# Moving the direct columns of a row pair from behind to ahead of its second bf16 products

## Chip, cores, metric

One core of one Trainium2 chip. The metric is the device time of one execution in microseconds.

## The reference, cut to what matters

```python
def reference(x, w_qkv):              # x: (16, 512, 768) f32, w_qkv: (768, 2304) f32
    qkv = np.matmul(x, w_qkv)
    ...                               # q, k, v = thirds of the last axis
    return np.stack([q, k, v], axis=0)
```

So it is one matrix product of 8192 x 768 by 768 x 2304, stored in another arrangement.

## The kernel before

The rows are worked in 32 pairs of 128-row blocks; "pair" below means such a pair of row blocks. After three pairs of start-up, 28 pairs go through `two` and the last one through `last`. Of the 2304 columns, 2048 are two "quads" (`a` and `b`: a pair of row blocks by a pair of 512-column blocks), computed by a Winograd form of Strassen's scheme with seven block products instead of eight. The remaining 256 are the "direct columns", computed plainly by `rem`. Products 1 and 2 run in bf16; products 3 to 7 use f32 operands made of sums (`float32r`).

```python
def product(u, n, ps, start):                  # three matmuls of 512 columns
    ...
    for j in range(KH):                        # KH = 3
        nc.tensor.matmul(ps[:], lhs[j], rhs[j], start=(start and j == 0), ...)

def do(u, n):
    ...
    if n == 1:
        u.x = bank(); product(u, 1, u.x, True)
        nc.scalar.activation(c11, u.x[:], ident)
    elif n == 2:
        u.z = bank(); product(u, 2, u.z, True)
        nc.vector.tensor_tensor(c11, c11, u.z[:], op=add)
    elif n == 6:
        product(u, 6, u.x, False)              # adds to product 1
        nc.scalar.activation(c12, u.x[:], ident)
    ...

def rem_row(p, r, ps):                         # six matmuls of 256 columns
    for j in range(KT):
        nc.tensor.matmul(ps, xb[p][:, j, r * P:(r + 1) * P], w_rem[:, j, :], ...)

def rem(p):                                    # the direct columns of a pair
    ps = ps_pool.tile([P, 2, REM], fp32, name="ps")
    for r in range(2):
        rem_row(p, r, ps[:, r, :])
    o = or_pool.tile([P, 2, REM], fp32, name="orem")
    nc.scalar.activation(o[:], ps[:], ident)
    nc.sync.dma_start(rows_of(1, p, R_OFF - H, R_OFF - H + REM), o[:])

def two(a, b, early):
    do(a, 1); do(b, 1)
    early()                                    # next pair: transpose, cast, sums; loads of the one after
    do(a, 2); do(b, 2)
    rem(a.p)
    do(a, 6); do(b, 6)
    do(a, 5); do(a, 7); do(b, 5); do(b, 7)
    do(a, 4); do(a, 3); store_quad(a)
    do(b, 4); do(b, 3); store_quad(b)
```

On TensorE a pair is therefore 12 bf16 matmuls of 512 columns, 12 bf16 matmuls of 256 columns and 30 f32 matmuls of 512 columns.

## Time and profile before

| | before |
|---|---|
| median time, first three runs | 363.31 us (363.23 to 363.45) |
| span of the profile | 362.0 us |
| TensorE busy | 98% |
| period of a pair in the steady loop | 10.76 us |
| the 54 matmuls of a pair at their own steps (a step: from one matmul's start to the next one's) | 10.70 us |

The views that carry the argument are shown in the prediction. Beside them belongs the table by stretches, here two pairs of the loop. Its columns are the stretch, its length, then for each engine the busy time with the number of instructions, the granted clock, the DMA's busy share and GB/s.

```profile
206.87:217.63 10.76, 10.69 (x54) 7.83 (x55) 6.78 (x8) 5.38 (x9) 5.86 (x6) 1.00 0.95 294
217.63:228.39 10.76, 10.69 (x54) 7.82 (x55) 6.77 (x8) 5.39 (x9) 5.85 (x6) 1.00 0.90 293
```

TensorE fills 10.69 of 10.76 us, and every pair looks like the next one. VectorE, ScalarE and GpSimd have 4 to 5 us free in each. ScalarE's idle time stands ahead of these evictions (groups of instructions: count, busy us and mean ns, idle us before them with what ended it):

```profile
L266 ACT ACTIVATE orem<-ps 128x512 f32<-128x512 f32 x31 | 18.6, 601 | 56.3 <-PE ps L256 54.3
...
L227 ACT ACTIVATE o<-ps 128x512 f32<-128x512 f32 x58 | 34.7, 599 | 6.6 <-PE ps L206 1.5
```

L266 evicts the direct columns and waits for TensorE 54.3 us in all.

### The profile page before, as it was taken

The page shows a single profiled execution, that of the slowest core. Times are in us where ns is not written, and L with a number is a line of the kernel's source. Part 1 is how long each engine was busy: PE and PEld are TensorE (multiplying, and loading weights), DVE is VectorE, ACT ScalarE, POOL GpSimd, SP SyncE. Part 2 cuts the span into 40 slices and gives each one's busy share as a digit, 9 for nine tenths or more (in the row PEclk, how much of TensorE's full clock was granted, in tenths as well). Part 3 has the DMA queues.
Part 4 walks back from the last instruction along what each step waited for, and adds up shares of the span by engine and source line. Part 5 has one row for each costly group of instructions (what it writes and reads, how often), then busy time and mean ns, then how long its engine had stood idle before and what let it go on. Part 6 is the DMA issues. An engine that isn't in the chain of part 4 may idle for free.

```text
span 362.0 us, 5220 instructions
## 1 busy us (share of the span) xinstructions
PE 353.5 (98%) x1765; PEld 248.6 (69%) x1797; DVE 224.4 (62%) x239; ACT 182.5 (50%) x304; POOL 174.1 (48%) x180
## 2 busy tenths in 40 slices
PE   8999999999999999999999999999999999999995
PEld 3644577777777776777777777777777777777763
DVE  3489746865566765566675565676556676556642
ACT  4547554445454545454545544444545454545452
POOL 0000960756664445664445665444666444666410
PEclk9999999999999999999999999999999999999999
DMA  7999969999999989899899999899989998989766
GB/s 295 381 381 339 346 224 343 331 304 298 278 321 298 295 275 295 282 313 313 284 277 294 281 306 316 281 283 285 295 284 317 295 295 274 300 275 332 266 251 242
DMA packets 80617, 108.08 MB, mean 299 GB/s; under 512 B 4816, under 2 KB 60368, under 8 KB 80592
## 3 DMA queue, kind: packets, MB, share of 16 engines
q1 hardware_dynamic: 65184, 96.35, 82.5%
q10 hardware_dynamic: 15408, 11.41, 9.7%
q8 instruction: 14, 0.23, 0.3%
q14 instruction: 11, 0.09, 0.1%
HBM read 32.24 MB, written 75.50 MB: 298 GB/s over the span
## 4 chain that ended last, share of the span: by engine, by line
PE 96%; ACT 1%; issue 1%; ACTq 0%; DVE 0%
PE ps L206 75%; PE ps L256 11%; PE ps L382 9%; PE ps L362 1%; PE ps L161 1%; ACT o L237 0%; ACTq L297 0%; ACT xb L141 0%; ACT orem L311 0%; DVE xb L139 0%; ACT xc L141 0%; ACTq L313 0%; DVE zero L340 0%; ACTq L311 0%
## 5 line engine op out<-in xcount | busy, mean ns | idle before, releaser
L206 PE MATMUL ps<-t,s 128*128 128x512 f32 x696 | 171.4, 395 | 0.0
L206 PEld LDWEIGHTS ps<-t,s 128*128 128x128 f32 x696 | 128.5, 188 | 26.5
L169 POOL CAST xb<-xf 128x1536 bf16<-128x1536 f32 x29 | 43.9, 1514 | 168.5 <-DVE xf L124 159.1
L234 DVE TENSOR_TENSOR o<-o,ps 128x512 f32<-128x512 f32 x58 | 39.9, 689 | 91.8 <-ACT o L233 91.8
L124 DVE STREAM_TRANSPOSE xf<-xin 128x1536 f32<-128x1536 f32 x29 | 85.5, 2950 | 5.7 <-DMA xin<-in_x_dram 2.9
L206 PE MATMUL ps<-b,xb 128*128 128x512 bf16 x320 | 74.2, 379 | 1.9
L206 PEld LDWEIGHTS <-xb 128*128 128x128 bf16 x348 | 31.7, 98 | 41.6 <-issue 7.3
L233 ACT ACTIVATE o<-ps 128x512 f32<-128x512 f32 x58 | 34.7, 598 | 44.7 <-PE ps L206 44.7
L240 DVE TENSOR_TENSOR o<-o,ps 128x512 f32<-128x512 f32 x58 | 39.9, 688 | 21.4 <-PE ps L206 20.2
L206 PE MATMUL ps<-b,s 128*128 128x512 f32 x174 | 48.7, 389 | 0.0
L256 PE MATMUL ps<-w_rem,xb 128*128 128x256 bf16 x384 | 47.2, 273 | 0.0
L266 ACT ACTIVATE orem<-ps 128x512 f32<-128x512 f32 x31 | 18.6, 601 | 56.3 <-PE ps L256 54.3
L237 ACT ACTIVATE o<-ps 128x512 f32<-128x512 f32 x58 | 34.7, 598 | 24.2 <-PE ps L206 21.4
L220 ACT ACTIVATE o<-ps 128x512 f32<-128x512 f32 x58 | 34.6, 597 | 23.8 <-DVE o L240 20.7
L256 PEld LDWEIGHTS <-xb 128*128 128x128 bf16 x384 | 37.4, 98 | 11.2 <-issue 0.5
L227 ACT ACTIVATE o<-ps 128x512 f32<-128x512 f32 x58 | 34.7, 599 | 6.6 <-PE ps L206 1.5
L224 DVE TENSOR_TENSOR o<-o,ps 128x512 f32<-128x512 f32 x58 | 36.4, 668 | 2.0 <-ACT o L220 1.3
L206 PEld LDWEIGHTS ps<-b,s 128*128 128x128 f32 x174 | 32.6, 188 | 6.9
L178 POOL TENSOR_TENSOR s<-s,xf 128x384 fp32r<-128x384 f32 x29 | 30.1, 1039 | 2.3
L177 POOL TENSOR_TENSOR s<-xf 128x384 fp32r<-128x384 f32 x29 | 31.0, 1069 | 0.0
L179 POOL TENSOR_TENSOR s<-xf 128x384 fp32r<-128x384 f32 x29 | 29.5, 1017 | 0.0
L181 POOL TENSOR_TENSOR s<-xf,s 128x384 fp32r<-128x384 f32 x29 | 29.5, 1016 | 0.0
(36 smaller groups left out, 129.3 us busy)
## 6 DMA issues: line engine op xcount, KB each, us to landing
out_dram<-o SPq DMA_DIRECT2D x62, 768.0 KB, 5.3
out_dram<-o SPq DMA_DIRECT2D x65, 256.0 KB, 4.5
xin<-in_x_dram SPq DMA_DIRECT2D x62, 192.0 KB, 6.7
xin<-in_x_dram ACTq DMA_DIRECT2D x54, 192.0 KB, 4.5
out_dram<-orem SPq DMA_DIRECT2D x31, 256.0 KB, 5.1
st<-in_w_qkv_dram SPq DMA_DIRECT2D x6, 768.0 KB, 14.1
xin<-in_x_dram SPq DMA_DIRECT2D x3, 768.0 KB, 5.7
st<-in_w_qkv_dram SPq DMA_DIRECT2D x6, 256.0 KB, 6.2
```

Source lines behind the costliest of these rows:

```text
L124: nc.vector.transpose(t[:].rearrange("p j (g b) -> p g j b", b=G), xin.pop(p)[:].rearrange("p g (a j) -> p g j a", a=G),)
L169: nc.gpsimd.tensor_copy(out=xb[p][:], in_=xf[p][:])
L206: nc.tensor.matmul(ps[:], lhs[j], rhs[j], start=(start and j == 0), stop=(j == KH - 1), skip_group_check=True,)
L220: nc.scalar.activation(c11, u.x[:], ident)
L224: nc.vector.tensor_tensor(c11, c11, u.z[:], op=add)
L227: nc.scalar.activation(c12, u.x[:], ident)
L233: nc.scalar.activation(c22, u.x[:], ident)
L234: nc.vector.tensor_tensor(c22, c22, u.y[:], op=add)
L237: nc.scalar.activation(c21, u.x[:], ident)
L240: nc.vector.tensor_tensor(c12, c12, u.y[:], op=add)
L256: nc.tensor.matmul(ps, xb[p][:, j, r * P:(r + 1) * P], w_rem[:, j, :], start=(j == 0), stop=(j == KT - 1), skip_group_check=True,)
L382: nc.tensor.matmul(ps[n][:], xb[p][:, j, r * P:(r + 1) * P], w[:, j, :], start=(j == 0), stop=(j == KT - 1), skip_group_check=True,)
```

## The change

The direct columns go between the first and the second bf16 products. One line moves:

```diff
         do(a, 1)
         do(b, 1)
         early()
+        rem(a.p)
         do(a, 2)
         do(b, 2)
-        rem(a.p)
         do(a, 6)
         do(b, 6)
```

Its intent can be read as twofold. The direct columns' eviction falls into a time when ScalarE has nothing to do. And the f32 products then follow wide matmuls instead of narrow ones.

## The prediction

> **What bounds the kernel now.** I read the busy shares first, then the chain that ended last, then the costliest groups, then one pair of the steady loop instruction by instruction. The page, first and fourth part:
>
> ```profile
> PE 353.5 (98%) x1765; PEld 248.6 (69%) x1797; DVE 224.4 (62%) x239; ACT 182.5 (50%) x304; POOL 174.1 (48%) x180
> ...
> PE 96%; ACT 1%; issue 1%; ACTq 0%; DVE 0%
> PE ps L206 75%; PE ps L256 11%; PE ps L382 9%; PE ps L362 1%; PE ps L161 1%; ACT o L237 0%; ACTq L297 0%; ACT xb L141 0%; ACT orem L311 0%; DVE xb L139 0%; ACT xc L141 0%; ACTq L313 0%; DVE zero L340 0%; ACTq L311 0%
> ```
>
> TensorE is busy 98% of the 362.0 us span, and 96% of the chain that sets the end is TensorE's own work; L206 are the products, L256 the direct columns. The other engines have a third to a half of their time free. Busy does not yet mean that no time is lost, so I look at the weight loads and matmuls by form:
>
> ```profile
> L206 PE MATMUL ps<-b,xb 128*128 128x512 bf16 x320 | 74.2, 379 | 1.9
> L206 PEld LDWEIGHTS <-xb 128*128 128x128 bf16 x348 | 31.7, 98 | 41.6 <-issue 7.3
> L256 PE MATMUL ps<-w_rem,xb 128*128 128x256 bf16 x384 | 47.2, 273 | 0.0
> L206 PEld LDWEIGHTS ps<-t,s 128*128 128x128 f32 x696 | 128.5, 188 | 26.5
> ```
>
> The 379 and 273 ns are latencies, with ends that are modelled; what counts is the step from start to start. Also 348 weight loads stand against 320 matmuls: 28 records are missing, one in each of the 28 pairs that the change touches, and the 0.26 us of "issue" idle at each pair's first weight load is that missing matmul, not a stall. One pair on TensorE in the timeline, from its first recorded bf16 product to the next pair's:
>
> ```profile
> 206.87 2.54 PE L206 MATMUL ps<-b,xb 128*128 128x512 bf16 x11
> 209.24 1.47 PE L256 MATMUL ps<-w_rem,xb 128*128 128x256 bf16 x12
> 210.47 5.05 PE L206 MATMUL ps<-t,s 128*128 128x512 f32 x21
> 215.35 0.84 PE L206 MATMUL ps<-b,s 128*128 128x512 f32 x3
> 216.03 0.84 PE L206 MATMUL ps<-t,s 128*128 128x512 f32 x3
> 216.72 0.84 PE L206 MATMUL ps<-b,s 128*128 128x512 f32 x3
> 217.62 0.38 PE L206 MATMUL ps<-b,xb 128*128 128x512 bf16 x1
> ```
>
> Start to start: bf16 512 columns (209.24-206.87)/11 = 0.2155 us; by single starts 215.7 ns. Direct columns 109 ns each. f32 matmuls 226.7 ns (the last ones, 0.68 us for three). A pair has 12, 12 and 30 of them: 12 x 215.7 + 12 x 109.1 + 30 x 226.7 = 10,699 ns. The pair's period, 217.62-206.87, is 10.76 us, and single starts give 10,760 ns for every pair from the fifth to the 31st. So **62 ns of a pair are not matmul stepping**, and no wait for another engine fits into that.
>
> **What the Trainium skill says.** "TensorE: Matmul & The Clock Gate", section "Back-to-back issue gap", gives N/2.4 + 2.5 ns for a warm matmul: 215.8 ns for 512 columns and 109.2 for 256. The trace agrees for bf16 (215.7 and 109); the f32 ones are 11 ns slower. The same page, "Step-by-step: what each phase is for", says that a weight load is pulled ahead of the running matmul, only the matmuls staying in order, so a load costs nothing while it fits under a matmul. Here a bf16 load is 98 ns, under the 109 ns of a direct column; an f32 load is 188 ns, under the 216 ns of a bf16 product but **not under the 109 ns of a direct column**. Its section "Weight-path perf modes" has the fast load for types other than FP32 only, which agrees with 98 against 188. "Perfetto Trace Analysis", "Identifying the Most-Contended Engine", warns that matmul busy time is no measure of headroom; hence the count above.
>
> **The change part by part.** Nothing is added or taken out: twelve direct-column matmuls (1.31 us a pair) go from behind the second bf16 products to ahead of them. Building both kernels and comparing their order shows that on ScalarE, VectorE, GpSimd and the DMA queue the order stays the same; only TensorE's differs, and PSUM banks are dealt out in another order. The order of data types on TensorE is bf16 then f32 before and after: the number of switches stays. What changes is the neighbour at the switch: an f32 product now follows a 512-column matmul, not a 256-column one.
>
> What is the present switch worth? In the pair above the last direct column starts at 210.44 and the second f32 matmul at 210.78: 340 ns, against 109 + 227 = 336, so about 5 lost. Then the next f32 steps are slow; the timeline cut to two windows shows it:
>
> ```profile
> 210.78 2.24 PE L206 MATMUL ps<-t,s 128*128 128x512 f32 x9
> ...
> 212.63 2.89 PE L206 MATMUL ps<-t,s 128*128 128x512 f32 x12
> ```
>
> From 210.78 to 212.63 are 8 steps of 231 ns; from 212.63 to 215.35 are 12 steps of 226.7. By single starts the switch and the slow steps after it cost 46 ns a pair, the switch back to bf16 some 14, which accounts for the 62. The last pair has its own order and shows the other switch, from 512 columns of bf16 to f32, at 349.64:
>
> ```profile
> 350.29 0.39 PE L206 MATMUL ps<-t,s 128*128 128x512 f32 x1
> ...
> 350.52 0.61 PE L206 MATMUL ps<-t,s 128*128 128x512 f32 x2
> ...
> 350.75 3.11 PE L206 MATMUL ps<-t,s 128*128 128x512 f32 x13
> ```
>
> There the third f32 matmul starts at 350.29, the steps are 231, then 226.7 from 350.75 on: 14 ns in all. So the gain can be up to 46 - 14 = 32 ns a pair, 0.9 us over 28 pairs (an estimate). I don't take it whole: the slow steps look like a phase between weight loads and matmuls that settles after 3 steps here and after 9 there, and where the new order enters that phase I can't tell. **I take three quarters, 0.7 us: 363.31 - 0.7 = 362.6 us.**
>
> On the other engines one sees work move with no effect on the path. The eviction of the direct columns (0.60 us on ScalarE) is now ready 1.3 us earlier, in 1.96 us that ScalarE idles today. The additions of the second products are ready later, but VectorE is still transposing then:
>
> ```profile
> 207.44 2.94 DVE L124 STREAM_TRANSPOSE xf<-xin 128x1536 f32<-128x1536 f32 x1
> 210.30 1.25 DVE L224 TENSOR_TENSOR o<-o,ps 128x512 f32<-128x512 f32 x2
> ```
>
> After the change the products of the first quad start their last matmul at some 209.7 and end at 210.1, before the transpose frees VectorE at 210.3; those of the second quad end at 210.7, before the second addition starts at 210.9. Neither starts later than now.
>
> **The rivals.** First, a bank wait takes the gain and more: the direct columns now claim a bank 1.3 us earlier. Were it held by the second quad's eviction of the first product (until 208.79), TensorE would stall 0.85 us a pair, 24 us in all, 387 us. Against it: the built program's waits. The direct columns have no bank wait of their own; the second quad's second product waits for an eviction of the pair before, over by 205.4, four microseconds ahead. "PSUM — Partial Sum Buffer", "PSUM bank collisions raise a hardware error", makes such waits the program's duty, so a bank without one is free by an earlier wait. I give this under 2%. Second, the slow f32 steps come not from the neighbour but from GpSimd's cast, which begins at 210.45, at the same moment, or from VectorE: then nothing changes, 363.3 us. For it, the coincidence; against it, the last pair's switch from direct columns to f32 is followed by slow steps (231 ns mean) with no GpSimd work left. A third of the chance lies here or in a full settling from the new entry. Third, VectorE falls behind (its slack for the second quad is only 0.15 us) and delays its evictions: these have microseconds before TensorE needs the banks, so still 363.3. Fourth, the DMA, 90 to 95% busy in the loop, becomes the bound: the bytes are the same, and the store of the direct columns stays queued behind the input's issue until 211.7. So no change.
>
> **Range and chances.** The whole gain gives 362.4, none 363.3; run to run the kernel spreads over 0.2 us, and another chip may shift all by some tenths. Range 361.9 to 363.4. A gain of 2% would be 7.3 us, more than four times all the 62 ns leftovers together (1.7 us), so it is out of reach; a loss of 2% needs 260 ns of stall in each pair, which only the first rival makes.
>
> **What the profile will show.** If right: no idle on TensorE in the pairs, a period of about 10.73 us, and the step from the last bf16 product to f32 followed by fewer slow f32 steps than 9; VectorE's additions still start as the transpose ends. If the second rival holds, the period stays at 10.76 with the slow steps in the same place. Wrong would be a pause of TensorE ahead of the direct columns, or a period above 10.8.

## The result and the profile after

A ratio here is the mean time of one kernel's fast runs over that of the other's in the same rounds, so it is not quite the ratio of the quoted medians.

| | before | after |
|---|---|---|
| median, first session | 363.34 us (363.23 to 363.90, 6 runs) | 363.09 us (362.67 to 363.44, 6 runs) |
| ratio, first session | | 0.9990 (95%: 0.9977 to 1.0003) |
| ratio, second session (last experiment) | | 0.9988 (0.9974 to 1.0002) |
| span of the profile | 362.0 us | 361.4 us |
| period of a pair | 10.76 us | 10.74 us |

At 2% the two are the same. The timed runs alone do not separate them: both intervals just contain 1. The traces do. The page after, busy shares and chain:

```profile
PE 353.3 (98%) x1765; PEld 250.8 (69%) x1797; DVE 222.7 (62%) x239; ACT 182.5 (51%) x304; POOL 174.4 (48%) x180
...
PE 96%; ACT 1%; issue 1%; ACTq 0%; DVE 0%
```

Nothing has moved between engines. One pair on TensorE after (start us, length us, instruction, count):

```profile
206.27 1.47 PE L206 MATMUL ps<-b,xb 128*128 128x512 bf16 x6
207.58 1.47 PE L256 MATMUL ps<-w_rem,xb 128*128 128x256 bf16 x12
208.89 1.46 PE L206 MATMUL ps<-b,xb 128*128 128x512 bf16 x5
209.99 5.14 PE L206 MATMUL ps<-t,s 128*128 128x512 f32 x21
214.97 0.84 PE L206 MATMUL ps<-b,s 128*128 128x512 f32 x3
215.65 0.84 PE L206 MATMUL ps<-t,s 128*128 128x512 f32 x3
216.33 0.84 PE L206 MATMUL ps<-b,s 128*128 128x512 f32 x3
217.01 1.47 PE L206 MATMUL ps<-b,xb 128*128 128x512 bf16 x6
```

From 206.27 to 217.01 are 10.74 us. The direct columns follow the first six products without a gap: 207.58 - 206.27 is six bf16 steps (1.295 us) and some 11 ns that the switch from f32 adds behind its first matmul. The missing matmul record now lies among the second products (5 of 6), which supports reading it as a lost record and not as a stall. The second trace of this kernel (e12) settles it: it has all 348 bf16 products, where this one has 320, and the same period. The timeline cut behind the switch to f32, as for the kernel before:

```profile
210.63 1.09 PE L206 MATMUL ps<-t,s 128*128 128x512 f32 x4
...
211.79 3.34 PE L206 MATMUL ps<-t,s 128*128 128x512 f32 x14
```

The second f32 matmul starts at 210.41. Then come six unsettled steps ("unsettled" are the steps behind the switch until they stay at 226.7 ns), to 211.79, averaging 230 ns; the 14 steps from 211.79 to 214.97 are 227. Before, there were nine.

By single starts (each matmul's start read from the trace on its own) the unsettled steps together cost 22 ns beyond 226.7 each, against 41 before. The step across the switch itself costs 3 to 4 ns, against 5. That is the whole 20 ns of the pair. Over 28 pairs it makes 0.56 us of the 0.63 us by which the two spans differ.

ScalarE and VectorE in the changed kernel:

```profile
L266 ACT ACTIVATE orem<-ps 128x512 f32<-128x512 f32 x31 | 18.6, 598 | 22.7 <-PE ps L256 21.4
...
L227 ACT ACTIVATE o<-ps 128x512 f32<-128x512 f32 x58 | 34.8, 600 | 40.0 <-PE ps L206 37.3
```

```profile
207.07 2.94 DVE L124 STREAM_TRANSPOSE xf<-xin 128x1536 f32<-128x1536 f32 x1
209.93 1.25 DVE L224 TENSOR_TENSOR o<-o,ps 128x512 f32<-128x512 f32 x2
```

33 us of ScalarE's waiting moved from ahead of the direct columns' eviction (L266) to ahead of product 6's (L227), and the time did not care. VectorE's additions still start where the transpose ends.

### The profile page after: what moved, and what is told of

Read it like the earlier page. It is cut to its first block, busy times and chain, and to the rows that moved or that the text cites. A ratio compares the mean times of both kernels' runs of the same rounds, so it can differ in the third digit from the quotient of the medians.

```text
span 361.4 us, 5220 instructions
## 1 busy us (share of the span) xinstructions
PE 353.3 (98%) x1765; PEld 250.8 (69%) x1797; DVE 222.7 (62%) x239; ACT 182.5 (51%) x304; POOL 174.4 (48%) x180
## 4 chain that ended last, share of the span: by engine, by line
PE 96%; ACT 1%; issue 1%; ACTq 0%; DVE 0%
PE ps L206 75%; PE ps L256 11%; PE ps L382 9%; PE ps L362 1%; PE ps L161 1%; ACT o L237 0%; ACTq L297 0%; ACT xb L141 0%; ACT orem L311 0%; DVE xb L139 0%; ACT xc L141 0%; ACTq L313 0%; DVE zero L340 0%; ACTq L311 0%
## 5 line engine op out<-in xcount | busy, mean ns | idle before, releaser
L206 PE MATMUL ps<-t,s 128*128 128x512 f32 x696 | 173.8, 398 | 0.0
L206 PEld LDWEIGHTS ps<-t,s 128*128 128x128 f32 x696 | 130.7, 188 | 29.8
L169 POOL CAST xb<-xf 128x1536 bf16<-128x1536 f32 x29 | 46.4, 1601 | 167.7 <-DVE xf L124 167.7
L206 PE MATMUL ps<-b,xb 128*128 128x512 bf16 x320 | 82.4, 380 | 1.5
L227 ACT ACTIVATE o<-ps 128x512 f32<-128x512 f32 x58 | 34.8, 600 | 40.0 <-PE ps L206 37.3
L266 ACT ACTIVATE orem<-ps 128x512 f32<-128x512 f32 x31 | 18.6, 598 | 22.7 <-PE ps L256 21.4
L179 POOL TENSOR_TENSOR s<-xf 128x384 fp32r<-128x384 f32 x29 | 29.5, 1017 | 0.0
L177 POOL TENSOR_TENSOR s<-xf 128x384 fp32r<-128x384 f32 x29 | 29.3, 1012 | 0.0
```

Of the source, the lines that this page charges most:

```text
L169: nc.gpsimd.tensor_copy(out=xb[p][:], in_=xf[p][:])
```

## The experiments

The question was what sets the unsettled f32 steps, since the whole difference lies there. Theory N says the width of the matmul just ahead of the first f32 product does. It is the prediction's own reason. Theory G says GpSimd's cast beside them does. Theory P says only the moment at which the f32 chain is entered does. Each edit is against the kernel before unless it says otherwise.

### e1: the next pair's preparation issued later

```diff
-        early()
         do(a, 2)
         do(b, 2)
         rem(a.p)
+        early()
         do(a, 6)
```

> Kernel before, with the block that transposes, casts and sums the next pair's input (VectorE, GpSimd) issued after the direct columns instead of before the second products; TensorE's order stays that of before. Theory N (the narrow matmul just ahead of the first f32 product sets the slow f32 steps): they stay where they are, some 9 of about 231 ns, period 10.76 us. Rival G (GpSimd's cast or VectorE beside them slows the f32 steps): they move with the cast, by some 3 us, or vanish, and the period falls towards 10.72. Time within 0.3% of 363.3 us for both.

Measured: 375.34 us, ratio 1.0331 (1.0316 to 1.0346), a period of about 11.16 us. So the time missed both expectations. The timelines of TensorE, GpSimd and ScalarE in one pair:

```profile
206.27 5.44 PE L206 MATMUL ps<-t,s 128*128 128x512 f32 x21
```

```profile
202.33 1.01 POOL L181 TENSOR_TENSOR s<-xf,s 128x384 fp32r<-128x384 f32 x1
209.03 1.46 POOL L169 CAST xb<-xf 128x1536 bf16<-128x1536 f32 x1 [5.68 <-DVE xf L124]
```

```profile
206.55 1.38 ACTq L120 DMA_DIRECT2D xin<-in_x_dram  x2
207.98 1.09 ACT L227 ACTIVATE o<-ps 128x512 f32<-128x512 f32 x2 [0.83 <-PE ps L206]
```

GpSimd is idle from 203.3 to 209.03. Yet the f32 steps from 206.6 to 208.2 are the usual unsettled ones (229, 234, 235, 225, 230, 236, 229 ns by single starts). **Theory G falls for GpSimd.** VectorE was transposing at that time, so for VectorE this run says nothing; the trace of before does (below the table).

The 3% come from elsewhere. The two input loads that ScalarE issues now stand ahead of the evictions of product 6. ScalarE sits idle for 0.83 us before the first of these (the profile puts this down to TensorE, but product 6 was over by some 207.2), and TensorE, which adds product 7 to the same bank, waits some 0.3 us once a pair (a step of 527 ns in place of 227). It then enters a second unsettled stretch. That the loads' issue is the reason is read from the order of times; it was not tried alone.

### e2: direct columns first in the pair

```diff
+        rem(a.p)
         do(a, 1)
         do(b, 1)
         early()
         do(a, 2)
         do(b, 2)
-        rem(a.p)
         do(a, 6)
```

> Direct columns at the very start of the pair, ahead of the first bf16 products; the matmul ahead of f32 is a 512-column one as in the changed kernel, six of them or more. Theory N: period 10.74 us as in the changed kernel. Rival P (only a phase, set by all that comes before, decides how many slow steps there are): any number from 10.71 to 10.77. If the switch from f32 into narrow matmuls is dear (the last pair shows 230 and 120 ns against 227 and 109, 14 ns, as into wide ones), 10.74 still.

Measured: period 10.740 us, six unsettled steps, as theory N said. But the time was 364.62 us, ratio 1.0042 (1.0026 to 1.0059), slower than before. The loop is not to blame. The first pair lost time once:

```profile
65.91 0.93 PE L206 MATMUL ps<-b,s 128*128 128x512 f32 x3 [1.65 <-DVE o L234]
```

In that pair the next input's loads were issued from 55.15, behind the direct columns' store in the same queue. Before, they were issued from 53.12, ahead of it. The transpose started at 60.92 instead of 59.58, VectorE's additions slipped behind it, and TensorE waited for one of them.

### e3: direct columns between the second product of the first quad and that of the second

```diff
         do(a, 2)
+        rem(a.p)
         do(b, 2)
-        rem(a.p)
```

> Direct columns between the second product of the first quad and that of the second quad: three 512-column matmuls still stand ahead of f32. Theory N: period 10.74 us, the same settling of f32 steps as in the changed kernel. Rival P: another number of slow steps, 10.71 to 10.77.

Measured: 362.83 us, ratio 0.9987 (0.9973 to 1.0002), period 10.740 us, six unsettled steps. This is the changed kernel over again, as theory N said. It is not told apart from the changed kernel. Theory P allowed anything from 10.71 to 10.77, so neither e2 nor e3 speaks against it.

### e4: direct columns among the f32 products

```diff
-        rem(a.p)
         do(a, 6)
         do(b, 6)
+        rem(a.p)
         do(a, 5)
```

> Direct columns among the f32 products: two more switches of data type. Theory N: the changed kernel's 10.74 us plus a switch into bf16 (14 ns) and a switch from a 256-column matmul to f32 (36 to 46 ns): 10.79 to 10.80 us, 1.4 to 1.7 us more than the changed kernel over 28 pairs, 0.3% slower than before at most. Rival (switches cost nothing and the slow steps belong to the place in the pair): 10.74 to 10.76.

Measured: 364.18 us, ratio 1.0024 (1.0009 to 1.0039), and a period of 10.79 us. The direct columns of two pairs in the timeline:

```profile
210.59 1.48 PE L256 MATMUL ps<-w_rem,xb 128*128 128x256 bf16 x12
...
221.39 1.49 PE L256 MATMUL ps<-w_rem,xb 128*128 128x256 bf16 x12
```

By single starts the period is 10.793 or 10.794 us: two more switches of type cost 53 ns over the changed kernel. The size fits theory N, but one detail does not. Behind these narrow matmuls, the same twelve as in the kernel before, there were six unsettled steps, not nine. And the other switch of the pair, behind 512 columns, lost 11 ns across it (453 ns), not 3.

### e5 to e8: one matmul of zeros added just ahead of the f32 products

These four keep the order of everything else and change the neighbour, at the price of one more matmul and one more bank in the rotation. The added matmul reads zeros and writes a bank that nobody reads. Results stay correct.

```diff
+    def filler(n):
+        ps = bank()
+        nc.tensor.matmul(ps[:, :n], zero[:, :P], zero[:, :n], start=True, stop=True)
 ...
         rem(a.p)
+        filler(512)      # e5; e6: filler(384)
         do(a, 6)
```

e7 and e8 do the same to the changed kernel, behind `do(b, 2)`, with `filler(256)` and `filler(128)`.

> Kernel before with one more 512-column bf16 matmul (of zeros, into a bank of its own that nobody reads) between the direct columns and the first f32 product. Theory N (the width of the last matmul ahead of f32 decides): period 10.760 + 0.216 - 0.020 = 10.956 us, six slow f32 steps. Rival (twelve direct columns anywhere near the switch, or the place in the pair, decide): 10.976 us and nine slow steps.

> As the run before with 384 columns (162 ns by the same stepping), less than the 188 ns of an f32 weight load. Theory N with a sharp threshold at the weight load: the narrow form of the switch, 10.760 + 0.162 = 10.922 us. Theory N without a sharp threshold: between 10.902 and 10.922.

> The changed kernel with one 256-column matmul of zeros between the second products and the first f32 product. Theory N: one narrow matmul is enough, 10.740 + 0.109 + 0.020 = 10.869 us and nine slow steps. Rival (it takes the run of twelve): 10.849 us and six slow steps.

> The changed kernel with one 128-column matmul of zeros (56 ns by the same stepping) there. The f32 weight load sticks out by 132 ns instead of 79. Theory N, cost growing with what sticks out: more than 10.740 + 0.056 + 0.020 = 10.816 us, perhaps 10.83 to 10.87. Rival: 10.796 us.

Each was profiled and timed once: 369.31, 367.73, 366.08 and 365.57 us, beside 363.23 us for the kernel before. The periods can be read at the added matmul (e5, then e7):

```profile
213.30 0.38 PE L271 MATMUL ps<-zero 128*128 128x512 bf16 x1
224.27 0.38 PE L271 MATMUL ps<-zero 128*128 128x512 bf16 x1
```

```profile
211.46 0.27 PE L271 MATMUL ps<-zero 128*128 128x256 bf16 x1
222.30 0.27 PE L271 MATMUL ps<-zero 128*128 128x256 bf16 x1
```

e5 has a wide neighbour and still nine unsettled steps. Its 10.973 us are close to the rival's 10.976. e7 has a narrow neighbour and two unsettled steps. Its 10.840 us are below both expectations. e6 (10.920) and e8 (10.840) fit values given for theory N, but with nine and two unsettled steps, so not by its reasoning. **Theory N falls as the reason for the unsettled steps.**

What the neighbour itself costs would show in the step across the switch. From the start of the last bf16 matmul to that of the second f32 one are 445 ns behind 512 columns in e5 and 391 to 392 behind 384, which is 2 to 3 above plain stepping. Behind 256 columns it is 341 to 342, which is 5 to 6 above. Behind 128 columns it is 343, which is some 60 above (with 56 ns taken for such a matmul, an estimate from the steps of 256 and 512 columns). So what the 188 ns load lacks under its neighbour (79 ns behind 256 columns, 132 behind 128, in the terms of theory N) is not what is lost. Nor is it the width alone: behind 512 columns e4 lost 11 ns.

### e9 to e11: the added matmul cut by 8 or 10 columns, or put elsewhere

All periods so far, except that of e1 with its stall, are multiples of 6.67 ns: 10.740, 10.760, 10.793, 10.840, 10.920 and 10.973 us are 1611, 1614, 1619, 1626, 1638 and 1646 times 6.667 ns. Theory P takes that as a grid onto which the f32 chain settles, at a cost that depends on where the chain is entered. The matmuls of zeros in e5 and e6 had happened to lengthen the pair by whole grid steps (213.3 and 160.0 ns between the periods). A few columns fewer should then change the number of unsettled steps.

```diff
-        filler(512)      # e5
+        filler(504)      # e9;  e10: filler(502)
```

e11 puts `filler(504)` into the changed kernel between the first products and `rem`, far from the switch.

> The wide-fill kernel with 504 columns of zeros instead of 512, 3.3 ns less of work; it is still wider than a weight load. Theory N (width of the neighbour; already in doubt, since the wide fill kept nine slow steps): 10.973 - 0.003 = 10.970 us and nine slow steps. Theory P (what counts is the moment at which the f32 chain is entered, on a grid of 6.67 ns that all periods so far lie on): the entry moves by half a grid step, to where the changed kernel's lies: six slow steps, 23 ns instead of 40, period 10.953 us.

> 502 columns, 4.2 ns less than with 512. Theory N: 10.969 us and nine slow steps. Theory P: the entry falls where that of the kernel with the narrow fill lies: two slow steps, 11 ns instead of 40, period 10.940 us.

> The changed kernel with 504 columns of zeros between the first products and the direct columns, far from the switch; the six matmuls ahead of f32 are the same wide ones. Theory N: 10.740 + 0.212 = 10.952 us and six slow steps. Theory P: the entry is shifted to three eighths of the grid as in the narrow fill: two slow steps, 10.940 us.

Measured: 368.80, 368.50 and 369.48 us (one run each). The periods at the added matmul, e9 and then e10:

```profile
213.04 0.38 PE L271 MATMUL ps<-zero 128*128 128x504 bf16 x1
223.99 0.38 PE L271 MATMUL ps<-zero 128*128 128x504 bf16 x1
```

```profile
212.92 0.38 PE L271 MATMUL ps<-zero 128*128 128x502 bf16 x1
223.86 0.38 PE L271 MATMUL ps<-zero 128*128 128x502 bf16 x1
```

By single starts 10.953 and 10.940 us, both where theory P put them. **3.3 ns less work takes 20 ns off the pair, and 4.2 ns less takes 33 ns off**, with a neighbour that stays wide. The unsettled steps were four in e9 (six were expected) and two in e10, against nine in e5. For e11 the period, 10.953, is the one given for theory N and not P's 10.940, but it had four unsettled steps where N said six. My working of where its entry would fall was wrong. The run does show that the number changes from six to four while the six matmuls ahead of f32 stay the same; what the steps cost hardly changed, 21 ns against 22.

| kernel | columns ahead of f32 | last bf16 start to second f32 start, ns | unsettled steps | their cost, ns | period, us |
|---|---|---|---|---|---|
| before | 256 | 341 | 9 | 41 | 10.760 |
| after, e2, e3 | 512 | 445 to 446 | 6 | 22 to 23 | 10.740 |
| e4, the longer f32 chain | 256 | 342 | 6 | 22 | 10.793 |
| e5 | 512 | 445 | 9 | 41 | 10.973 |
| e6 | 384 | 391 to 392 | 9 | 41 | 10.920 |
| e7 | 256 | 342 | 2 | 10 | 10.840 |
| e8 | 128 | 343 | 2 | 10 | 10.840 |
| e9 | 504 | 445 | 4 | 21 | 10.953 |
| e10 | 502 | 443 | 2 | 10 | 10.940 |
| e11 | 512 | 448 | 4 | 21 | 10.953 |

**The unsettled steps of all these runs are one sequence, entered at different places.** Before it is 229, 233, 236, 224, 231, 236, 228, 233, 231 ns, then 227. After the change it is the last six of these, in e9 the last four, in e10 the last two, each to within 1 ns; the other runs agree within 2. This is what a phase would look like, and it explains why four steps can cost as much as six: 224 is below the settled step.

The trace of the kernel before holds a further case, in the last pair (TensorE, then VectorE):

```profile
354.51 0.94 PE L206 MATMUL ps<-t,s 128*128 128x512 f32 x3
```

```profile
354.07 0.69 DVE L234 TENSOR_TENSOR o<-o,ps 128x512 f32<-128x512 f32 x1 [0.67 <-ACT o L233]
356.19 1.37 DVE L240 TENSOR_TENSOR o<-o,ps 128x512 f32<-128x512 f32 x2 [1.43 <-PE ps L206]
```

Here too f32 follows 256-column matmuls, and the steps from 354.83 to 356.21 are 231, 230, 236, 229, 232, 231 ns: six unsettled ones, while VectorE is idle from 354.76 to 356.19 and GpSimd has no work left. **So theory G falls for VectorE as well.**

Theory P needs one reservation. The recorded start of the second f32 matmul does not tell how many steps will follow: in e5, e9 and e11 it comes equally long after the last f32 start of the pair before (4,585.8 ns), yet nine, four and four steps follow. What e9 and e10 show is that 3 or 4 ns of work decide; that they do so through the moment of entry is argued, because the recorded starts do not show that moment.

### e12: the changed kernel timed again

The kernel is the changed one, with no edit.

> The changed kernel once more, timed in five rounds against the one before. The two profiles' periods differ by 20 ns, 0.56 us over 28 pairs: 0.15% faster, ratio 0.9985, some 362.75 us beside 363.3. Rival (the profile's gain does not reach the clock on the wall): ratio 1.000.

Measured: 362.89 us (362.77 to 363.16, 5 runs) beside 363.33 (363.20 to 363.96, 9 runs), ratio 0.9988 (0.9974 to 1.0002). The centre is where the traces put it, and the interval still reaches 1. Its trace again has a period of 10.740 us, here with no matmul record of the pairs missing.

No version beat the changed kernel by more than the runs can tell. An entry as lucky as that of e10 would save 11 to 12 ns a pair, 0.3 us in all (an estimate from the table), but every matmul added to get it cost more than that.

## Why the prediction was right or wrong

**Time: right.** It put 362.6 us in a range from 361.9 to 363.4; 363.09 and 362.89 us were measured. The gain it took, 0.7 us, is 0.56 us in the pairs by the trace and 0.25 to 0.44 us between the medians. The range also held the 363.3 us of no gain at all, so the time alone tested little.

**TensorE's steps alone bound the loop: right.** The period changed only by what the f32 steps gave back, and no wait came up. The lost records, read as such, moved with the order.

**Nothing moves on the other engines' path: right.** The additions start as the transpose ends, at 209.93. ScalarE's eviction of the direct columns came earlier, at 209.23 against 210.75. Of these 1.52 us, 0.38 are the changed trace's lead at this pair, so it gained 1.14 us and not the 1.3 that its data did. By the order of times it now waited for ScalarE's own issue of the input loads, which ends at 209.12.

**The switch from narrow to f32 costs 46 ns, from wide to f32 14, because of the neighbour: this step failed.** The sum of the parts was sound: 46 became 26, not 14. The cause was not. A wide neighbour with nine unsettled steps (e5), a narrow one with two (e7), and the same twelve narrow ones with nine and with six (before, e4) refute it. An f32 load of 188 ns over a direct column of 109 lost 5 ns at the switch, not the 79 by which it is longer. Of the 20 ns gained, 2 lie in the step across the switch, and even these are not shown to come from the width. The other 18 come from a later entry into the same sequence of unsettled steps: e9 and e10 took 3 and 4 ns from the added matmul, still wide, and the period fell by 20 and 33. The prediction's own trace held the warning: behind narrow direct columns its last pair has six unsettled steps, and behind wide products (from 349.64) two, where the changed kernel then showed six. That the loop gained three units of 6.67 ns, and not more or none, was not foreseeable from the trace of before. The prediction's caution, that it could not tell where the new order enters such a phase, was the sound part. That three quarters of a gain with the wrong cause came out near was luck.

**The rivals.** The bank wait did not come: the direct columns start 109 ns stepping at once. GpSimd's cast is refuted by e1, and VectorE as a cause of the unsettled steps by the last pair of the trace of before. VectorE did not run late, and the DMA did not bind.

**Open** is what the grid of 6.67 ns is, why the chain takes up to nine steps to settle on it, and what sets the place at which the sequence is entered. The runs show that it is there, not what makes it. That the columns taken away in e9 and e10 act by their time, and not in another way, was not tried apart. e11 also shows that I cannot yet compute the entry for an arbitrary order.

## What to carry to other kernels

When the bound engine's own steps add up to the period, reordering work on it can win only what is lost at the switches between kinds of work; count that first, since here it was 62 of 10,760 ns. A coincidence of a slow stretch with one neighbour is not a cause: add one matmul of the other kind and look again. Moving work on a full engine still moves other queues with it, and that is where the losses were. By the order of times, loads issued from ScalarE ahead of a needed eviction cost 3% (e1), and a store queued ahead of the input's load cost 1.65 us at once (e2).

## What the Trainium skill lacked or had wrong

- "TensorE: Matmul & The Clock Gate", "Back-to-back issue gap": it gives some 131 ns for each matmul of 512 columns in a stream with a weight load for each. Here, with a load for each, 512 bf16 columns step at 215.8 ns and 256 at 109.2, which is its formula for the isolated gap. That formula names no operand type; f32 products of 512 columns step at 226.7 ns once settled.
- Same page, "LDWEIGHTS (loading the stationary operand)": columns divided by 1.2 gives 107 ns for 128 columns. The trace has 98 ns for bf16 and 188 ns for f32.
- No page has the cost of going from bf16 to f32 matmuls: 340 to 343 ns from the start of the last bf16 matmul to that of the second f32 one behind 256 columns and no less behind 128, and then in the loop two to nine steps of 224 to 236 ns in place of 226.7, costing 10 to 41 ns together; nor the 6.67 ns of which all stall-free periods were multiples.
